# Two halves of the columns, two blocks of rows apart, in the second product of an MLP

## The chip, the cores and the metric

The kernel runs on one core of a Trainium2 chip. The metric is the time of one execution in device microseconds: 2081.96 us is the median of three runs (2080.67 to 2084.63).

## The reference, cut to what matters

The program is one encoder layer with 512 tokens and 2048 features, in float32: neighbourhood attention, and then an MLP, each behind an RMS norm and added to its input. The change touches the last line of the MLP only.

```python
def sq_relu_mlp(h, w1, w2):        # h: 512 x 2048, w1: 2048 x 8192, w2: 8192 x 2048
    a = jax.nn.relu(h @ w1)
    return (a * a) @ w2

x = x + sq_relu_mlp(rms_norm(x, norm_mlp[layer]), mlp_w1[layer], mlp_w2[layer])
```

## The kernel before, in words

Both products of the MLP are done in *units*, objects of class `Pair`. A unit makes 512 tokens x 1024 columns (two tiles of 512 columns) from four *blocks* of 512 rows of the weight. Each block is a 2 x 2 multiplication of quarters that is done with seven products instead of eight (the Strassen-Winograd scheme); the seven are numbered 1, 5, 6, 4 (first stage) and 2, 3, 7 (second stage). `Pair.chunks` gives the order: first stage of all blocks, then second stage of all blocks, 28 steps for four blocks. Each step takes one weight quarter of 128 x 1024 values and one *left side*, a combination of quarters of the left matrix. Both are kept as two float32r parts, a high one and the rest (h and l), and a step is 12 matmuls of 128 x 512: four places times hh, hl and lh (L248).

What a step needs of the other engines:

- The weight quarter (512 KB) is loaded by SP six steps ahead (`load_raw`, L193) into one of ten buffers. VectorE adds an earlier quarter for products 5, 6, 4 and 7 (L217). ScalarE makes the high part (L233) and VectorE the rest (L235), started three steps ahead.
- Products are summed in PSUM. When the last block of a product is done, `evict` takes its two banks to SBUF and adds the parts together (L265 to L274, L670, L672).

There are eight units h0 to h7 for the first product, and then eight for the second: y0_0, y0_1, y1_0, y1_1, y2_0, y2_1, y3_0, y3_1. The first number is one of four groups of four blocks (2048 rows of w2), the second is the half of the columns, called p. So both halves of the columns go through the same four blocks, one after the other.

The left sides of the second product are made from the hidden units' results. `take_hidden` scales and applies ReLU; eight *windows* of work follow in the next unit, one behind each second-stage step. A window transposes four squares on TensorE, ScalarE squares them, VectorE makes sums (L714 to L719), and POOL's queue writes them to DRAM (`z_t`, seven left sides of a block). `pass_on` brings them back: behind a step (m, b) of a unit, when the left side that this step used is not needed again, SP loads one left side (256 KB, L759, `zr`), and six sub-steps later (a step has four) ScalarE and VectorE split it (L554, L556). Before the change this is done in h7, y0_1, y1_1 and y2_1, for all 28 left sides of the next group; y0_0, y1_0, y2_0 and the units of group 3 make none. So 56 tiles of 128 x 512 hold left sides all the time, of 70 that the pool has.

A unit of the second product ends in eight quarters of 128 x 512. `take_out` lets POOL's queue add each of them into `y_sum` in DRAM with an accumulating DMA (L748). Only the last unit of either half loads `y_sum` (L732, called from the step with product 4 of the last block), adds it and writes the output.

The order of the work on each engine follows the program's order of issue: `later` and `start` put the side work of a step behind a number of sub-steps, and every engine and SP's queue work in order.

Of the kernel before, what the change touches and what calls it, by code (L numbers as in the profile page):

```python
# [17 lines left out]
P = 128  # L18
T = 512
D = 2048  # L20
# [5 lines left out]
NCH = HID // D  # L26
# [6 lines left out]
NB = KT // 4  # L33
# [8 lines left out]
STEP, WAIT, PAIR = 1, 5, 3  # L42


class Unit:
# [7 lines left out]
    def __init__(self, name, src, act, done, kind):  # L53
        self.name, self.src, self.act, self.done, self.kind = name, src, act, done, kind
        self.n = KT // 4 if kind == "narrow" else KT
        self.raw, self.parts, self.ps = {}, {}, None
        self.load, self.before, self.after, self.lag = None, None, None, 0


class Pair:  # L60
# [16 lines left out]
    QUARTER = {1: (0, 0), 5: (0, 1), 6: (1, 1), 4: (1, 0), 2: (1, 0), 3: (1, 1), 7: (0, 1)}  # L77
    CHAIN = {5: 1, 6: 5, 4: 6, 7: 3}

    def __init__(self, name, w, row, col, comb, take):  # L80
        self.name, self.w, self.row, self.col, self.comb, self.take = name, w, row, col, comb, take
        self.raw, self.parts, self.banks, self.after = {}, {}, {}, None
        self.t, self.u, self.p4, self.p5 = {}, {}, {}, {}

    def chunks(self):
        return [(self, (m, b)) for stage in (self.FIRST, self.SECOND) for b in range(NB) for m in stage]

    def quarter(self, m, b):
        r, c = self.QUARTER[m]
        r, c = self.row + (4 * b + 2 * r) * P, self.col + c * T  # L90
        return self.w[r // (2 * P), c // T]


# [1 line left out]
def natten_mlp_kernel(ctx, tc, x_t, gains, w_qk, w_v, bias, w_o, w1, w2, out_t):  # L95
    nc = tc.nc
# [8 lines left out]
    def wtile(name, dt=F32):  # L105
        return tiles.tile([P, T], dt, tag="w", name=name)

    def bank(name):
        return psum.tile([P, T], F32, tag="b", name=name)
# [11 lines left out]
    def pair(name):  # L121
        return wtile(f"{name}h", F32R), wtile(f"{name}l", F32R)
# [49 lines left out]
    def later(lag, fn):  # L172
        side.append((pos[0] + lag, fn))

    def start(steps):

        wait = next(steps, None)
        if wait is not None:
            later(wait, lambda: start(steps))

    def run_side(until):
        while True:
            due = sorted((s for s in side if s[0] <= until), key=lambda s: s[0])
            if not due:
                return
            for s in due:
                side.remove(s)
                s[1]()
# [48 lines left out]
    def multiply_pair(u, i):  # L237
        m, b = i
        x = u.BANK[m]
        if x not in u.banks:  # L240
            u.banks[x] = [bank(f"{x}_{u.name}_{j}") for j in range(2)]
        wh, wl = u.parts.pop(i)
        ah, al = u.comb[b][m]
        for k in range(2):
            for j in range(2):
                c = slice(k * HALF + j * P, k * HALF + (j + 1) * P)
                for n, (a, w) in enumerate(((ah, wh), (ah, wl), (al, wh))):
                    nc.tensor.matmul(out=u.banks[x][j], lhsT=a[:, c], rhs=w[:, k],  # L248
                                     start=(m in u.FIRST and b + k + n == 0), stop=(b == NB - 1 and k == 1 and n == 2),
                                     skip_group_check=True)  # L250
                pos[0] += 1
                if 2 * k + j < 3:
                    run_side(pos[0])
        if b == NB - 1:
            start(evict(u, m))
        if u.after is not None:
            u.after(m, b)
        run_side(pos[0])
# [148 lines left out]
    def v_done(g):  # L407
        def done(ps):
            vs[g] = [split(ps[j], f"v{g}_{j}", gain=r_mix[:, j:j + 1]) for j in range(QB)]
        return done  # L410

    class Head:
        def __init__(self, h):
            self.h = h
            self.p = {}
# [105 lines left out]
    for g in range(NG):  # L521
        u = Unit(f"v{g}", lambda i, g=g: w_v[i // 2, g], xa, v_done(g), "tokens")
# [24 lines left out]
    xc = [{} for _ in range(NB)]  # L547
    sq_a = wtile("sq_a")

    def parts_of(dst, m, src, name):  # L550

        h, l = pair(name)
        view = lambda z: z.rearrange("p (k n) -> p k n", k=2)
        nc.scalar.activation(view(h), src, AF.Copy)  # L554
        yield STEP
        nc.vector.tensor_tensor(out=view(l), in0=src, in1=view(h).bitcast(F32), op=ALU.subtract)  # L556
        dst[m] = (h, l)
        yield STEP
# [45 lines left out]
    def window():  # L604
        if windows:
            windows.pop(0)()
# [49 lines left out]
    for g in range(NG):  # L656
        u = Unit(f"o{g}", lambda i, g=g: w_o[i // 2, g], oa, o_done(g), "wide")
# [6 lines left out]
    FP = HID // (2 * T)  # L664

    z_t = [dram.tile([P, 7, 2, HALF], F32, name=f"z_{i}", tag=f"z_{i}") for i in range(2 * FP)]
# [8 lines left out]
    def take_hidden(p):  # L675
        zs = {}

        def take(c, half, src, add, minus=False):
            if add is None:
                t = wtile(f"z_{p}_{c}_{half}")  # L680
            else:
                t = join(src, add, minus)
                src = t
            nc.scalar.activation(t, src, AF.Relu, scale=r_a[:, c:c + 1])
            zs[c, half] = t
            if len(zs) == 8:
                for n in range(8):
                    windows.append(left_window(p, n // 4, n // 2 % 2, n % 2, zs))
        return take
# [35 lines left out]
    def take_out(p, last):  # L725
        ys = {}

        def prefetch():
            for c in range(QB):
                for half in range(2):  # L730
                    ys[c, half] = wtile(f"ys_{p}_{c}_{half}")
                    nc.sync.dma_start(out=ys[c, half], in_=y_sum[c, 2 * p + half])  # L732

        def take(c, half, src, add, minus=False):
            rows, cols = slice(c * P, (c + 1) * P), slice((2 * p + half) * T, (2 * p + half + 1) * T)
            if add is not None:
                if last:
                    nc.vector.tensor_tensor(out=add, in0=add, in1=ys[c, half], op=ALU.add)
                t = join(src, add, minus)
            elif last:  # L740
                t = join(src, ys[c, half], False)
            else:
                t = wtile(f"c_{p}_{c}_{half}")
                nc.scalar.activation(t, src, AF.Copy)
            if last:
                nc.sync.dma_start(out=out_t[rows, cols], in_=t)
            else:
                nc.gpsimd.dma_start(out=y_sum[c, 2 * p + half], in_=t, accum_op=ALU.add)  # L748
        return take, prefetch

    def pass_on(dst, block):


        order = (2, 4, 1, 5, 6, 3, 7)
        loaded = {}

        def load(m, b):
            t = loaded[m, b] = wtile(f"zr{m}_z{block}_{b}")
            nc.sync.dma_start(out=t.rearrange("p (k n) -> p k n", k=2), in_=z_t[4 * block + b][:, order.index(m)])  # L759

        def split_left(m, b):
            yield from parts_of(dst[b], m, loaded.pop((m, b)).rearrange("p (k n) -> p k n", k=2), f"a{m}_z{block}_{b}")

        def after(m, b):
            load(m, b)
            later(6 * STEP, lambda: start(split_left(m, b)))
        return after

    pairs, comb = [], xc
    for p in range(FP):  # L770
        u = Pair(f"h{p}", w1, 0, 2 * p * T, comb, take_hidden(p))
        pairs.append(u)
    zc = [[{} for _ in range(NB)] for _ in range(NCH)]
    for c in range(NCH):
        for p in range(2):
            take, prefetch = take_out(p, c == NCH - 1)
            u = Pair(f"y{c}_{p}", w2, c * D, 2 * p * T, zc[c], take)
            u.prefetch = prefetch if c == NCH - 1 else None
            pairs.append(u)
    for n, u in enumerate(pairs):  # L780
        hand = None
        if n >= FP - 1 and (n - FP + 1) % 2 == 0 and n < len(pairs) - 1:
            block = (n - FP + 1) // 2
            hand = pass_on(zc[block], block)

        def after(m, b, n=n, u=u, hand=hand):
            if m in u.SECOND:
                if n == 0 and m == 2 and b == 0:
                    start(norm_a())
                window()  # L790
            if m == 4 and b == NB - 1 and n >= FP and u.prefetch is not None:
                u.prefetch()
            if hand is not None:
                hand(m, b)
        u.after = after
        chunks += u.chunks()
# [54 lines left out]
```

## Time and profile before

| | before |
|---|---|
| median of three runs | 2081.96 us |
| profiled execution | 2081.29 us, span 2079.5 us, granted clock 0.995 |
| TensorE busy | 2044.1 us (98%) |
| TensorE's weight load busy | 1684.3 us (81%) |
| VectorE busy | 1546.5 us (74%) |
| ScalarE busy | 1045.5 us (50%) |
| POOL busy | 116.7 us (6%) |
| HBM | 348 MB read, 50 MB written, 192 GB/s |

The span is from the first to the last instruction. Weight loads overlap matmuls. The time of the engines beside TensorE counts only where TensorE waits for them.

### The profile page before, as it was taken

How to read it: one execution, taken by the hardware profiler on the slowest of the kernel's cores; microseconds unless marked ns; L12 is line 12 of the kernel's file. 1: busy time of each engine (PE TensorE's matmuls, PEld its weight loads, DVE VectorE, ACT ScalarE, POOL GpSimd, SP SyncE). 2: the span in 40 equal slices, each digit the busy share in tenths (PEclk: the TensorE clock that was granted, in tenths of full speed). 3: DMA queues.
4: the chain of work that ended last, by engine and by line, in shares of the span. 5: the costliest groups of instructions: out<-in, count | busy, mean ns of one | idle time of the engine just before them, and what ended most of it. 6: DMA issues, size and time to landing. Idle time of an engine off the chain costs nothing. (4 is left out here: it accounts for less than half of the span.)

```text
span 2079.5 us, 25226 instructions
## 1 busy us (share of the span) xinstructions
PE 2044.1 (98%) x9330; PEld 1684.3 (81%) x9330; DVE 1546.5 (74%) x1884; ACT 1045.5 (50%) x1412; POOL 116.7 (6%) x166
## 2 busy tenths in 40 slices
PE   9999999999999999999999999999989999999998
PEld 7888888888888888888888888887877877778787
DVE  6674674774774469778878878798879778779786
ACT  6663563653663445544545545565445445346333
POOL 0000000000000000010110110100201011010000
PEclk9999999999999999999999999999999999999999
DMA  7222222222233346565866757778689598688874
GB/s 289 101 92 83 100 92 92 96 90 96 99 101 127 112 137 211 193 217 199 274 202 226 269 180 255 270 255 304 226 295 286 187 272 279 204 261 278 256 243 147
DMA packets 127900, 400.15 MB, mean 192 GB/s; under 512 B 15008, under 2 KB 15008, under 8 KB 127776
## 3 DMA queue, kind: packets, MB, share of 16 engines
q1 hardware_dynamic: 110736, 352.37, 50.3%
q0 software_dynamic: 16896, 46.15, 7.8%
q8 instruction: 73, 1.20, 0.2%
q14 instruction: 51, 0.42, 0.1%
q10 hardware_dynamic: 144, 0.02, 0.0%
HBM read 348.14 MB, written 50.33 MB: 192 GB/s over the span
## 5 line engine op out<-in xcount | busy, mean ns | idle before, releaser
L233 ACT ACTIVATE wh_h<-w_h 128x1024 fp32r<-128x1024 f32 x224 | 237.6, 1060 | 275.0 <-PE y_h L248 83.7
L233 ACT ACTIVATE wh_y<-w_y 128x1024 fp32r<-128x1024 f32 x224 | 236.5, 1059 | 234.2 <-PE y_y L248 69.0
L235 DVE TENSOR_TENSOR wl_h<-w_h,wh_h 128x1024 fp32r<-128x1024 f32 x224 | 272.8, 1221 | 77.4 <-ACT wh_h L233 76.7
L235 DVE TENSOR_TENSOR wl_y<-w_y,wh_y 128x1024 fp32r<-128x1024 f32 x224 | 271.0, 1219 | 24.5 <-ACT wh_y L233 24.0
L217 DVE TENSOR_TENSOR w_y<-w_y,w_y 128x1024 f32<-128x1024 f32 x128 | 156.1, 1220 | 70.9 <-DMA w_y<-in_w 68.1
L217 DVE TENSOR_TENSOR w_h<-w_h,w_h 128x1024 f32<-128x1024 f32 x128 | 155.1, 1219 | 42.9 <-DMA w_h<-in_w 42.8
L235 DVE TENSOR_TENSOR wl_o<-w_o,wh_o 128x1024 fp32r<-128x1024 f32 x32 | 39.1, 1223 | 58.7 <-ACT wh_o L233 58.6
L233 ACT ACTIVATE wh_o<-w_o 128x1024 fp32r<-128x1024 f32 x32 | 33.9, 1059 | 80.0 <-PE mm_o L302 66.2
L233 ACT ACTIVATE wh_q<-w_q 128x1024 fp32r<-128x1024 f32 x32 | 34.0, 1062 | 77.8 <-PE mm_q L302 30.2
L235 DVE TENSOR_TENSOR wl_q<-w_q,wh_q 128x1024 fp32r<-128x1024 f32 x32 | 39.2, 1225 | 43.6 <-ACT wh_q L233 42.3
L235 DVE TENSOR_TENSOR wl_k<-w_k,wh_k 128x1024 fp32r<-128x1024 f32 x32 | 39.1, 1222 | 37.9 <-ACT wh_k L233 37.9
L233 ACT ACTIVATE wh_k<-w_k 128x1024 fp32r<-128x1024 f32 x32 | 34.0, 1062 | 50.8 <-PE mm_q L302 31.1
L233 ACT ACTIVATE wh_v<-w_v 128x1024 fp32r<-128x1024 f32 x31 | 32.8, 1058 | 47.4 <-PE mm_v L302 23.4
L235 DVE TENSOR_TENSOR wl_v<-w_v,wh_v 128x1024 fp32r<-128x1024 f32 x31 | 37.9, 1223 | 23.0 <-ACT wh_v L233 22.6
L600 POOL DMA_DIRECT2D y<-x1t_0s x4 | 2.3, 583 | 770.1 <-ACT x1t_0s L599 770.1
L711 POOL DMA_DIRECT2D z<-zt x32 | 17.7, 553 | 453.0 <-ACT zt L706 452.9
L554 ACT ACTIVATE a_z_0h<-zr_z 128x512 fp32r<-128x512 f32 x28 | 17.6, 627 | 50.4 <-DMA zr_z<-z 48.5
L509 ACT ACTIVATE t<-t,st 128x256 f32<-128x256 f32 x64 | 32.0, 501 | 10.6 <-DVE st L505 10.6
L706 ACT ACTIVATE zt<-zt 128x512 f32<-128x512 f32 x64 | 37.1, 580 | 0.0
L248 PE MATMUL y_y<-wl_y,a_z_1h 128*128 128x512 f32 x64 | 26.6, 416 | 8.4 <-DVE wl_y L235 8.4
L248 PE MATMUL z_y<-wl_y,a_z_0h 128*128 128x512 f32 x64 | 26.7, 418 | 6.8 <-DVE wl_y L235 6.8
L554 ACT ACTIVATE a_z_3h<-zr_z 128x512 fp32r<-128x512 f32 x28 | 17.5, 626 | 29.6 <-DMA zr_z<-z 29.6
(1435 smaller groups left out, 6304.2 us busy)
## 6 DMA issues: line engine op xcount, KB each, us to landing
w_h<-in_w SPq DMA_DIRECT2D x224, 512.0 KB, 4.3
w_y<-in_w SPq DMA_DIRECT2D x224, 512.0 KB, 4.6
zr_z<-z SPq DMA_DIRECT2D x112, 256.0 KB, 5.3
w_q<-in_w_qk SPq DMA_DIRECT2D x32, 512.0 KB, 3.5
w_k<-in_w_qk SPq DMA_DIRECT2D x32, 512.0 KB, 3.5
w_o<-in_w_o SPq DMA_DIRECT2D x32, 512.0 KB, 3.5
w_v<-in_w_v SPq DMA_DIRECT2D x31, 512.0 KB, 3.5
z<-zt POOLq DMA_DIRECT2D x32, 256.0 KB, 3.9
```

Source lines behind the costliest of these rows:

```text
L217: nc.vector.tensor_tensor(out=s, in0=s, in1=u.raw[u.CHAIN[m], b], op=ALU.add)
L233: kept(nc.scalar.activation(h, s, AF.Copy))
L235: kept(nc.vector.tensor_tensor(out=l, in0=s, in1=h.bitcast(F32), op=ALU.subtract))
L248: nc.tensor.matmul(out=u.banks[x][j], lhsT=a[:, c], rhs=w[:, k], start=(m in u.FIRST and b + k + n == 0), stop=(b == NB - 1 and k == 1 and ...
L509: nc.scalar.activation(halves[i], halves[i], AF.Exp, bias=st[:, i:i + 1], accum_out=st[:, 2 + i:3 + i])
L554: nc.scalar.activation(view(h), src, AF.Copy)
L600: nc.gpsimd.dma_start(out=dst, in_=t)
L706: nc.scalar.activation(t[:, i], ps, AF.Square)
L711: nc.gpsimd.dma_start(out=dst[:, 2], in_=t[:, 0, :HALF])
```

## The change

`Pair` gets a range of blocks instead of a first row, so a unit may have any blocks. The second product has nine units y0 to y8. Even ones do p = 1, odd ones p = 0. y0 has blocks 0 and 1, y1 blocks 0 to 3, y2 blocks 2 to 5, y3 blocks 4 to 7, and so on to y7 with blocks 12 to 15 and y8 with 14 and 15. Each unit thus uses two blocks for the last time, and behind their steps the left sides of two new blocks are made. h7 makes those of blocks 0 to 3 as before, but the ones of blocks 2 and 3 come 48 sub-steps (12 steps) later. y1 to y6 make two blocks' each. y0 has six second-stage steps; behind the two with product 7 it runs a second window. The last unit of either half is y7 or y8.

```diff
-        return [(self, (m, b)) for stage in (self.FIRST, self.SECOND) for b in range(NB) for m in stage]
+        return [(self, (m, b)) for stage in (self.FIRST, self.SECOND) for b in self.blocks for m in stage]
...
-        if b == NB - 1:
+        if b == u.blocks[-1]:
             start(evict(u, m))
...
-    def pass_on(dst, block):
+    def pass_on(heirs):
...
         def load(m, b):
-            t = loaded[m, b] = wtile(f"zr{m}_z{block}_{b}")
-            nc.sync.dma_start(out=t.rearrange("p (k n) -> p k n", k=2), in_=z_t[4 * block + b][:, order.index(m)])
+            t = loaded[m, b] = wtile(f"zr{m}_z_{b}")
+            nc.sync.dma_start(out=t.rearrange("p (k n) -> p k n", k=2), in_=z_t[b][:, order.index(m)])
...
         def after(m, b):
-            load(m, b)
-            later(6 * STEP, lambda: start(split_left(m, b)))
+            if b in heirs:
+
+                wait = 48 * STEP if heirs[b] == b >= 2 else 0
+                later(wait, lambda: load(m, heirs[b]))
+                later(wait + 6 * STEP, lambda: start(split_left(m, heirs[b])))
         return after
...
+    pairs = [Pair(f"h{p}", w1, range(NB), 2 * p * T, xc, take_hidden(p)) for p in range(FP)]
+    zc = [{} for _ in range(NCH * NB)]
+    for n in range(2 * NCH + 1):
+        p, c = 1 - n % 2, 2 * n - 2
+        rows = range(max(c, 0), min(c + NB, NCH * NB))
+        take, prefetch = take_out(p, n >= 2 * NCH - 1)
+        u = Pair(f"y{n}", w2, rows, 2 * p * T, zc, take)
+        u.prefetch = prefetch if n >= 2 * NCH - 1 else None
         pairs.append(u)
-    zc = [[{} for _ in range(NB)] for _ in range(NCH)]
-    for c in range(NCH):
-        for p in range(2):
-            take, prefetch = take_out(p, c == NCH - 1)
-            u = Pair(f"y{c}_{p}", w2, c * D, 2 * p * T, zc[c], take)
-            u.prefetch = prefetch if c == NCH - 1 else None
-            pairs.append(u)
     for n, u in enumerate(pairs):
-        hand = None
-        if n >= FP - 1 and (n - FP + 1) % 2 == 0 and n < len(pairs) - 1:
-            block = (n - FP + 1) // 2
-            hand = pass_on(zc[block], block)
+        c = 2 * (n - FP) - 2
+        if n == FP - 1:
+            hand = pass_on({b: b for b in u.blocks})
+        elif n > FP and c + NB < NCH * NB:
+            hand = pass_on({c: c + NB, c + 1: c + NB + 1})
+        else:
+            hand = None
 
         def after(m, b, n=n, u=u, hand=hand):
             if m in u.SECOND:
                 if n == 0 and m == 2 and b == 0:
                     start(norm_a())
                 window()
+                if n == FP and m == 7:
+                    window()
```

## Rows read from the trace of the kernel before

**Rows 1.** The page, busy time of TensorE, share of the span, instructions.

```profile
PE 2044.1 (98%) x9330; PEld 1684.3 (81%) x9330; DVE 1546.5 (74%) x1884; ACT 1045.5 (50%) x1412; POOL 116.7 (6%) x166
```

**Rows 2.** Timeline of TensorE: first matmuls of h6, h7, y0_0 to y3_1; the last.

```profile
1258.54 0.39 PE L248 MATMUL x_h<-wh_h,a_x0h 128*128 128x512 f32 x1
...
1338.59 0.39 PE L248 MATMUL x_h<-wh_h,a_x0h 128*128 128x512 f32 x1
...
1419.65 0.39 PE L248 MATMUL x_y<-wh_y,a_z_0h 128*128 128x512 f32 x1
...
1502.18 0.39 PE L248 MATMUL x_y<-wh_y,a_z_0h 128*128 128x512 f32 x1
...
1587.89 0.39 PE L248 MATMUL x_y<-wh_y,a_z_0h 128*128 128x512 f32 x1
...
1667.71 0.39 PE L248 MATMUL x_y<-wh_y,a_z_0h 128*128 128x512 f32 x1
...
1753.54 0.39 PE L248 MATMUL x_y<-wh_y,a_z_0h 128*128 128x512 f32 x1
...
1834.07 0.39 PE L248 MATMUL x_y<-wh_y,a_z_0h 128*128 128x512 f32 x1
...
1918.59 0.39 PE L248 MATMUL x_y<-wh_y,a_z_0h 128*128 128x512 f32 x1
...
1997.16 0.39 PE L248 MATMUL x_y<-wh_y,a_z_0h 128*128 128x512 f32 x1
...
2073.29 0.39 PE L248 MATMUL y_y<-wh_y,a_z_3l 128*128 128x512 f32 x1
```

**Rows 3.** Windows: y0_1's first 43.5 us, its rest, and y1_0's first 43.5 us.

```profile
core 0: us, PE busy (x) PEld busy (x) DVE busy (x) ACT busy (x) POOL busy (x), PEclk, DMA share, GB/s
1502.20:1545.70 43.50, 36.67 (x151) 29.51 (x150) 34.09 (x38) 19.65 (x24) 3.90 (x5) 0.92 0.97 308
1545.70:1587.90 42.20, 42.20 (x188) 34.92 (x187) 40.44 (x47) 26.21 (x34) 1.72 (x2) 1.00 0.86 281
1587.90:1631.40 43.50, 41.35 (x181) 33.48 (x180) 32.54 (x33) 18.29 (x19) 5.27 (x6) 1.00 0.79 241
```

**Rows 4.** Waits (us in total, times, longest) from 1667.7 to 1711, start of y1_1.

```profile
ACT a_z_0h L554 <- DMA zr_z<-z: 12.2, 3, 7.7
DVE w_y L217 <- DMA w_y<-in_w: 5.4, 1, 5.4
...
PE z_y L248 <- DVE wl_y L235: 4.2, 1, 4.2
...
DVE a_z_0l L556 <- ACT a_z_0h L554: 3.6, 1, 3.6
```

**Rows 5.** Waits from 1587.9 to 1631, start of y1_0.

```profile
DVE w_y L217 <- DMA w_y<-in_w: 9.0, 3, 4.0
```

**Rows 6.** Transfers by queue from 1583 to 1606: packets, MB, share of 16 engines.

```profile
q1 hardware_dynamic: 1515, 4.71, 54.6%
q0 software_dynamic: 1152, 2.10, 52.1%
```

**Rows 7.** Transfers by queue from 1463 to 1502, windows' writes in y0_0.

```profile
q0 software_dynamic: 1066, 3.62, 25.0%
```

**Rows 8.** One instruction, min/median/max ns (first three); group of lines, busy us, mean ns.

```profile
L235 DVE TENSOR_TENSOR wl_y<-w_y,wh_y x224: 1210/1218/1228, 1418.6 to 2066.6; 128x1024 fp32r<-128x1024 f32 x112
L217 DVE TENSOR_TENSOR w_y<-w_y,w_y x128: 1212/1219/1227, 1410.7 to 2052.2; 128x1024 f32<-128x1024 f32 x128
...
L556 DVE TENSOR_TENSOR a_z_0l<-zr_z,a_z_0h x28: 677/684/693, 1346.5 to 1901.6; 128x512 fp32r<-128x512 f32 x28
...
L714 DVE TENSOR_TENSOR zt_0s<-zt 128x256 f32<-128x256 f32 x2 | 0.8, 419 | 0.0
```

**Rows 9.** Windows of 3 us in y0_1, columns as in rows 3.

```profile
1527.00:1530.00 3.00, 3.00 (x9) 2.33 (x8) 3.00 (x4) 1.49 (x2) 0.00 (x0) 0.50 0.88 326
```

More of the change, by code (lines that the diff above doesn't have):

```diff
@@ L78, with __init__ @@
     CHAIN = {5: 1, 6: 5, 4: 6, 7: 3}
-    def __init__(self, name, w, row, col, comb, take):
-        self.name, self.w, self.row, self.col, self.comb, self.take = name, w, row, col, comb, take
+    def __init__(self, name, w, blocks, col, comb, take):
+        self.name, self.w, self.blocks, self.col, self.comb, self.take = name, w, blocks, col, comb, take
         self.raw, self.parts, self.banks, self.after = {}, {}, {}, None
@@ L85, in chunks @@
     def chunks(self):
-        return [(self, (m, b)) for stage in (self.FIRST, self.SECOND) for b in range(NB) for m in stage]
+        return [(self, (m, b)) for stage in (self.FIRST, self.SECOND) for b in self.blocks for m in stage]
     def quarter(self, m, b):
         r, c = self.QUARTER[m]
-        r, c = self.row + (4 * b + 2 * r) * P, self.col + c * T
+        r, c = (4 * b + 2 * r) * P, self.col + c * T
         return self.w[r // (2 * P), c // T]
@@ L248, in multiply_pair @@
                     nc.tensor.matmul(out=u.banks[x][j], lhsT=a[:, c], rhs=w[:, k],
-                                     start=(m in u.FIRST and b + k + n == 0), stop=(b == NB - 1 and k == 1 and n == 2),
+                                     start=(m in u.FIRST and b == u.blocks[0] and k + n == 0),
+                                     stop=(b == u.blocks[-1] and k == 1 and n == 2),
                                      skip_group_check=True)
@@ L757, in load @@
         def load(m, b):
-            t = loaded[m, b] = wtile(f"zr{m}_z{block}_{b}")
-            nc.sync.dma_start(out=t.rearrange("p (k n) -> p k n", k=2), in_=z_t[4 * block + b][:, order.index(m)])
+            t = loaded[m, b] = wtile(f"zr{m}_z_{b}")
+            nc.sync.dma_start(out=t.rearrange("p (k n) -> p k n", k=2), in_=z_t[b][:, order.index(m)])
         def split_left(m, b):
-            yield from parts_of(dst[b], m, loaded.pop((m, b)).rearrange("p (k n) -> p k n", k=2), f"a{m}_z{block}_{b}")
+            yield from parts_of(zc[b], m, loaded.pop((m, b)).rearrange("p (k n) -> p k n", k=2), f"a{m}_z_{b}")
@@ L764, in after @@
         def after(m, b):
-            load(m, b)
-            later(6 * STEP, lambda: start(split_left(m, b)))
-        return after
-    pairs, comb = [], xc
-    for p in range(FP):
-        u = Pair(f"h{p}", w1, 0, 2 * p * T, comb, take_hidden(p))
-        pairs.append(u)
-    zc = [[{} for _ in range(NB)] for _ in range(NCH)]
-    for c in range(NCH):
-        for p in range(2):
-            take, prefetch = take_out(p, c == NCH - 1)
-            u = Pair(f"y{c}_{p}", w2, c * D, 2 * p * T, zc[c], take)
-            u.prefetch = prefetch if c == NCH - 1 else None
-            pairs.append(u)
@@ L790, in after @@
                 window()
-            if m == 4 and b == NB - 1 and n >= FP and u.prefetch is not None:
+                if n == FP and m == 7:
+                    window()
+            if m == 4 and b == u.blocks[-1] and n >= FP and u.prefetch is not None:
                 u.prefetch()
```

## The prediction

> **What bounds the kernel now.** I read the page's busy shares first, then TensorE's timeline at the start of each unit, then the windows inside the units, and last the waits and transfers at the places where time is lost. TensorE is busy for 98% of the span [rows 1], so only what TensorE loses can come back, and whatever makes it lose more is paid in full.
>
> The unit starts say where it loses [rows 2]. The last unit, y3_1, runs its 336 matmuls in 76.13 us from first to last start, 0.227 us each: 76.36 us is an undisturbed unit without transposes and 2.73 us one of its 28 steps (12 matmuls). The hidden unit h6, with 32 transposes among its matmuls, takes 80.05 us; that is the measure for h7 and y0_0, which have as many. Against these, the losses are: h7 1.0, y0_0 2.5, y0_1 9.35, y1_0 3.45, y1_1 9.45, y2_0 4.15, y2_1 8.15, y3_0 2.2, y3_1 0: together 40.3 us. That is all the change can win.
>
> The three units that make left sides behind an accumulating unit (y0_1, y1_1, y2_1) lose 9.0 us in the mean; the three that only follow an accumulating unit (y1_0, y2_0, y3_0) lose 3.3. The windows say when in the unit it happens [rows 3]: in the first 43.5 us of y0_1, TensorE starts 151 matmuls where 192 fit (43.5 / 0.227), and in the next 42.2 us 188, all that fit. Yet the left sides go on through both halves. So VectorE and the transfers keep up with 28 left sides in a unit; what fails is the first part of it. The DMA share there is 0.97, against 0.79 at the start of y1_0 [rows 3].
>
> There two things meet. The unit before leaves eight quarters of y, each added into DRAM by an accumulating DMA, and the first left sides are fetched. In y1_1 the waits are on transfers: ScalarE on `zr_z`, VectorE's join on a raw weight, and TensorE then on VectorE's split [rows 4]. In y1_0, without left sides to make, VectorE waits for weights too, 9.0 us in three waits [rows 5], and TensorE loses less.
>
> The transfers can be added up. In the 23 us around the start of y1_0 the accumulating queue moves exactly one unit's eight quarters, 2.10 MB, for 52.1% of the 16 engines' time, and SP's queue 4.71 MB for 54.6% [rows 6]. That is 5.7 us per MB and 2.67 us per MB. So one unit's accumulation costs 12.0 us of all 16 engines, one weight quarter (0.524 MB) 1.4 us, one left side (0.262 MB) 0.7 us. In the first eight steps (21.8 us) weights take 11.2 us and accumulation 12.0: 23.2, over by 1.4. With eight left sides, 5.6 more, it is 28.8, over by 7.0. The extra 5.6 us is what the two kinds of start differ by (9.0 - 3.3 = 5.7). When TensorE has stood still for long in such a start its clock falls to half, and the restart pays for that too: 9 matmuls in 3 us where 13 fit, at 0.50 of the clock [rows 9]; this is inside the 9.0.
>
> **The change, part by part.**
> *Units.* The p = 1 columns are cut into 2, 4, 4, 4 and 2 blocks, the p = 0 columns into four times 4, so nine units y0 to y8 replace eight. Matmuls, weights and left sides stay the same in number. One more unit is evicted and accumulated: 12 VectorE and 4 ScalarE instructions and 8 accumulating DMAs. They run beside TensorE, and what they cost is the one more unit start behind an accumulation, counted below. Without TensorE's cover the VectorE part would be 12 x 0.68 = 8 us.
>
> *Left sides.* What matters is where they stand. Every step of a block in `heirs` fetches one, and the heirs are the unit's first two blocks. In each of y1 to y6 the left sides are therefore made in steps 1 to 8 and 17 to 22. Steps 9 to 16 and 23 to 28 are freed, but these lose nothing now. In steps 1 to 8 stand just as many fetches as in the heavy units of before, eight, beside the same accumulation. The heavy start of y0_1, y1_1, y2_1 occurs six times (y1 to y6) instead of three. The light start occurs once (y7) instead of three times.
>
> I price a heavy start at 9.0 us, the mean of three rows. From below it is bounded by the light start, 3.3 (the left sides hidden), from above by 9.45 for y2 to y6. y1 may be worse, see the next paragraph. Six heavy starts are 54.0, y7 is 3.3, y8 follows a unit that writes straight to the output, as y3_1 does, and loses 0.
>
> *h7 and y0.* h7 now makes 22 left sides, because those of blocks 2 and 3 come 12 steps later. The other six fall on y0's steps 7 to 12. All 8 transposing windows of h7's result, one behind each of y0_0's first eight second-stage steps before, now stand in y0's six second-stage steps, two of them on the last. VectorE has there 8 splits and joins (9.8 us), 4 left sides (2.7), 16 window steps (6.7) and the first stage's 6 evictions (4.1), 23.3 us [rows 8], where TensorE needs 6 x 2.73 + 3.9 = 20.3. It falls 3 us behind. Three steps of prepared weights cover some of it; I take 2 us, between 0 and 6. The left-side and weight fetches stand on the same SP queue, so a fetch that waits for a free tile holds the weights behind it; that is the upper end. The 3.62 MB that the windows write cost a quarter of 39 us [rows 7], 9.8 us of the engines, and now end right at y1's start; y0_1 had some calm steps between. I leave y1 at 9.0 and keep +5 for the range. The losses of h7 (1.0) and y0's start (2.5) stay.
>
> *Waits and ends.* The change adds no wait to an instruction. A fetch still stands on SP behind the same step and the split on ScalarE six sub-steps later; behind that split on ScalarE are the weights' splits, for which VectorE and then TensorE wait, as in rows 4. At the end y8 has 14 steps. Its eight loads of y come six steps before the end instead of twelve, some 11 us before the first is used. I count 0, with 3 us as the other end if they arrive late.
>
> **The sum.** Losses after: 1.0 + 4.5 + 54.0 + 3.3 + 0 = 62.8 us, against 40.3: 22.5 us more. The profiled execution took 2081.3 us (span 2079.5), 0.7 us below the median of the runs, so the change should take 2103.8, about 2104 us.
>
> A rule speaks against this sum. The Trainium skill (DMA: Bandwidth & Descriptors, "Anatomy of one DMA") prices the moving part of a transfer as its bytes over 436 GB/s, whatever the kind. By that the first eight steps would carry 8.39 MB in an estimated 19.2 us, under 21.8, and a heavy start would lose nothing to transfers. The rows of this trace disagree for accumulating transfers (5.7 us per MB is 175 GB/s [rows 6]); the second rival has the time that would follow if the transfers were not the limit.
>
> **The rivals.**
> *The left sides' cost is kept, not doubled.* If each left side carries its own delay wherever it stands, 84 of them cost 3 x 5.7 = 17.1 us before and after. Then the light start is paid by seven units, 7 x 3.3 = 23.1, and with h7 and y0 at 3.5 the losses are 43.7: 3.4 us more, 2084.7. For it: the sum of fetched bytes is unchanged. Against it: the second half of y0_1 has 12 left sides and loses nothing [rows 3].
>
> *VectorE is the limit, and the change takes it off.* In a heavy first stage four steps cost 7 x 1.22 + 4 x 0.68 = 11.3 us on VectorE against 10.9 on TensorE [rows 8]; with half the left sides it is 9.9. If this, and not the transfers, makes the 9.0, all six middle units lose only what a light one does: 1.0 + 2.5 + 7 x 3.3 = 26.6, so 13.7 us less, 2067.6: faster. It decides if the first eight steps of y2 to y6 lose under about 5 us each (40.3 = 4.5 + 3.3 + 3.5 + 29, over six units). For it: TensorE's direct waits are on VectorE. Against it: in y1_1's start VectorE sits idle for a weight and for ScalarE [rows 4], and it keeps up in the second half of y0_1 [rows 3].
>
> *y0 and y1 pile up.* If VectorE's 3 us, tile waits and the late writes add up, y0 and y1 lose 6 and 14 instead of 4.5 and 9: 2110.
>
> **How the numbers follow.** Chances: the forecast 0.62, the pile-up on top of it 0.06, kept cost 0.13, VectorE 0.19. The forecast's own range is 2092 to 2113. To leave out no more than 2 in 10, I reach from 2072, which takes in the kept cost and half-way to VectorE's case, to 2116. What a measurement can tell from no change is 0.2%, about 4 us. The kept cost falls inside that for the most part; so faster 0.19, same 0.12, slower 0.69.
>
> **What would show it.** In the changed kernel's trace, TensorE's starts of y1 to y6 should be 84 to 87 us apart, each with its loss in the first eight or nine steps, a DMA share near 1 and a dip of the granted clock there. Steps 9 to 16 should be clean, and y7 near 79.6. ScalarE's waits on `zr_z` should about double. I am wrong if the middle units are 80 us long, if the losses move to other steps, or if y0 is far over 45 us.

## The result, and the profile after

The changed kernel takes 2107.8 us (median of four runs, 2105.8 to 2108.9), the kernel before 2083.15 us beside it: ratio 1.0118, 95% interval 1.0101 to 1.0136. It is slower by 1.2%. The forecast was 2104.0, between 2072 and 2116.

The profiled execution took 2108.9 us (span 2107.1), 27.6 us more than before's 2081.3. Here is TensorE's timeline with the first matmul of h7, y0 to y8, and the last matmul, as in [rows 2].

```profile
1341.19 0.39 PE L248 MATMUL x_h<-wh_h,a_x0h 128*128 128x512 f32 x1
1422.69 0.39 PE L248 MATMUL x_y<-wh_y,a_z_0h 128*128 128x512 f32 x1
1466.15 0.48 PE L248 MATMUL x_y<-wh_y,a_z_0h 128*128 128x512 f32 x1
1554.41 0.39 PE L248 MATMUL x_y<-wh_y,a_z_2h 128*128 128x512 f32 x1
1638.77 0.39 PE L248 MATMUL x_y<-wh_y,a_z_4h 128*128 128x512 f32 x1
1723.25 0.39 PE L248 MATMUL x_y<-wh_y,a_z_6h 128*128 128x512 f32 x1
1809.20 0.39 PE L248 MATMUL x_y<-wh_y,a_z_8h 128*128 128x512 f32 x1
1891.22 0.39 PE L248 MATMUL x_y<-wh_y,a_z_10h 128*128 128x512 f32 x1
1977.08 0.39 PE L248 MATMUL x_y<-wh_y,a_z_12h 128*128 128x512 f32 x1
2062.94 0.39 PE L248 MATMUL x_y<-wh_y,a_z_14h 128*128 128x512 f32 x1
2100.79 0.39 PE L248 MATMUL y_y<-wh_y,a_z_15l 128*128 128x512 f32 x1
```

Taking off 76.36 us for 28 steps, 38.18 for 14 and 3.7 for a unit's 32 transposes, as in the prediction, the losses are those in the second line of the table below. They add up to 65.2 us, against 40.3 before: 24.9 us more. The other 2.6 us stand ahead of h7 (it starts at 1341.19 instead of 1338.59), in code that is the same. Run e4, whose code up to there is that of before, starts h7 at 1341.19 too, so this is a difference between executions. Step by step, 56.0 of the 63.8 us that y0 to y8 lose fall in the first eight steps of a unit (before: 35.3 of 39.3).

Losses of TensorE in us, unit by unit, worked out for each run from the unit starts in its trace. The runs e1 to e10 are told below. The heads name the changed kernel's units; in brackets are those of the kernel before, for before, e4 and e8.

| kernel | h7 | y0 (y0_0) | y1 (y0_1) | y2 (y1_0) | y3 (y1_1) | y4 (y2_0) | y5 (y2_1) | y6 (y3_0) | y7 (y3_1) | y8 | sum |
|---|---|---|---|---|---|---|---|---|---|---|---|
| before | 1.0 | 2.5 | 9.35 | 3.5 | 9.5 | 4.2 | 8.2 | 2.2 | 0 | | 40.3 |
| after | 1.45 | 1.6 | 11.9 | 8.0 | 8.1 | 9.6 | 5.7 | 9.5 | 9.5 | 0 | 65.2 |
| e1 fetches later | 1.2 | 1.3 | 12.3 | 7.7 | 6.0 | 7.3 | 5.6 | 7.1 | 3.5 | 0 | 51.8 |
| e2 no left sides | 0.4 | 1.6 | 10.2 | 8.05 | 11.05 | 9.4 | 10.0 | 11.0 | 6.2 | 0 | 67.9 |
| e3 adds kept | 0.6 | 1.9 | 9.8 | 1.05 | 1.4 | 1.6 | 1.1 | 2.15 | 0 | 0 | 19.3 |
| e4 before, adds kept | 0.7 | 2.2 | 7.95 | 0.4 | 1.65 | 2.5 | 3.0 | 4.4 | 0 | | 22.5 |
| e5 adds kept, fetches later | 0.2 | 2.0 | 6.65 | 1.2 | 1.0 | 1.3 | 1.3 | 1.4 | 0 | 0 | 14.7 |
| e6 adds kept, split later | 0 | 0.7 | 7.6 | 0 | 0 | 0 | 0 | 0 | 0 | 0 | 7.1 |
| e7 plain writes | 1.2 | 1.05 | 7.4 | 3.1 | 3.6 | 3.2 | 4.0 | 3.6 | 3.1 | 0 | 30.2 |
| e8 before, both mends | 0 | 0.8 | 2.0 | 0.6 | 0 | 0.6 | 0 | 0.6 | 0 | | 4.0 |
| e9 split later alone | 0 | 0 | 5.2 | 7.7 | 6.5 | 9.2 | 6.2 | 9.2 | 4.6 | 0 | 48.2 |
| e10 all three | 0 | 0.65 | 1.0 | 0 | 0 | 0 | 0 | 0 | 0 | 0 | 0.3 |

(Values between -0.2 and 0.05 are written as 0; the sums are of the unrounded ones.)

One unit does not fit the prediction at all: y7. It makes no left sides, should have been a light start with 3.3 us, and lost 9.5. The waits of its first 43.5 us:

```profile
ACT wh_y L233 <- PE z_y L248: 14.4, 3, 7.0
DVE w_y L217 <- DMA w_y<-in_w: 10.9, 4, 5.9
...
PE z_y L248 <- DVE wl_y L235: 5.9, 2, 3.6
```

No left side is among them. VectorE stands 10.9 us for raw weights in the add of two quarters (L217). Its own timeline (start, length, what, idle before it and releaser) shows what this wait does:

```profile
1987.01 1.21 DVE L217 TENSOR_TENSOR w_y<-w_y,w_y 128x1024 f32<-128x1024 f32 x1
1988.14 1.22 DVE L235 TENSOR_TENSOR wl_y<-w_y,wh_y 128x1024 fp32r<-128x1024 f32 x1
1989.28 1.22 DVE L217 TENSOR_TENSOR w_y<-w_y,w_y 128x1024 f32<-128x1024 f32 x1
1996.43 1.22 DVE L217 TENSOR_TENSOR w_y<-w_y,w_y 128x1024 f32<-128x1024 f32 x1 [5.93 <-DMA w_y<-in_w]
1997.57 1.22 DVE L235 TENSOR_TENSOR wl_y<-w_y,wh_y 128x1024 fp32r<-128x1024 f32 x1
```

And SP's issue of the weight for which it waits, with the microseconds from that issue to its landing:

```profile
1987.11 0.33 SPq L193 DMA_DIRECT2D w_y<-in_w  x1
```

```profile
w_y<-in_w SPq DMA_DIRECT2D x1, 512.0 KB, 9.2
```

1987.11 + 9.2 = 1996.3: the add waits for a load that was issued 3.4 us before VectorE came to it (1996.43 - 5.93 = 1990.50). Yet SP has weights issued ten buffers ahead: at 1992 us, 27 loads and 37 splits (L235) are still to come. So the add is not for the weight that TensorE needs next, it is for one some eight steps later, and the split that TensorE needs stands behind it (1997.57). In VectorE's queue, counted in the order of the trace, the number of splits between an add and the split of the same weight, for the 16 adds of a unit in order, is:

```
before  y0_1   3 3 3 4 2 2 3 3 3 3 3 3 5 7 8 6
before  y1_0   7 7 7 7 7 7 4 4 5 6 6 6 8 8 8 8
before  y1_1   8 8 7 8 8 8 8 6 6 7 7 7 7 7 8 6
after   y1     4 4 3 1 1 1 1 1 1 1 1 2 4 6 8 7
after   y3     8 7 7 8 8 8 8 6 6 7 7 7 7 8 8 7
after   y7     8 7 7 8 8 8 8 6 6 8 8 7 8 8 8 6
e1      y3     7 7 7 7 7 8 6 6 6 7 7 7 8 8 8 6
e2      y3     8 8 7 8 8 8 8 6 6 8 8 7 8 8 8 8
e3      y3     1 1 1 1 1 1 1 1 1 1 1 1 1 1 3 4
e9      y3     7 7 7 8 8 8 5 5 5 6 6 6 8 8 8 7
```

The kernel's text issues an add three steps ahead; the scheduler that orders each engine's instructions had moved it up. I had read before's order of work from the text; what is said of it ahead of the prediction holds for the text alone. The waits of rows 4 and 5 on raw weights are waits of the same adds (L217). The light starts of before differ in this order too. VectorE at the start of y1_0:

```profile
1586.60 0.68 DVE L556 TENSOR_TENSOR a_z_2l<-zr_z,a_z_2h 128x512 fp32r<-128x512 f32 x1
1587.20 1.28 DVE L672 TENSOR_TENSOR u_y<-z_y,u_y 128x512 f32<-128x512 f32 x2
1588.40 1.21 DVE L235 TENSOR_TENSOR wl_y<-w_y,wh_y 128x1024 fp32r<-128x1024 f32 x1
...
1592.53 1.22 DVE L235 TENSOR_TENSOR wl_y<-w_y,wh_y 128x1024 fp32r<-128x1024 f32 x1
...
1594.26 1.22 DVE L235 TENSOR_TENSOR wl_y<-w_y,wh_y 128x1024 fp32r<-128x1024 f32 x1
...
1596.00 1.21 DVE L235 TENSOR_TENSOR wl_y<-w_y,wh_y 128x1024 fp32r<-128x1024 f32 x1
1597.14 1.21 DVE L217 TENSOR_TENSOR w_y<-w_y,w_y 128x1024 f32<-128x1024 f32 x1
```

From 1586.6 to 1597.1, while the accumulation starts, four splits go by without an add between them. In y1_0 and y1_1 alike, the first six adds are done before the unit starts. The seventh stands four splits ahead of its own in y1_0 and comes 9.3 us into the unit; in y1_1 it stands eight ahead and comes after 4.9 us, in y2_1 after 3.3, and in y2 to y7 of the changed kernel after 2.7 to 4.6. Why the scheduler orders one unit this way and another that way is not shown.

Two units are of another kind: y0_1 before and y1 after, whose first adds stand only one to four ahead (table). Lines from the waits of their first 43.5 us, y0_1 first:

```profile
ACT a_z_0h L554 <- DMA zr_z<-z: 14.6, 3, 11.0
...
PE y_y L248 <- ACT wh_y L233: 5.6, 1, 5.6
```

```profile
ACT a_z_4h L555 <- DMA zr_z<-z: 15.3, 3, 7.6
...
PE w_y L248 <- ACT wh_y L233: 4.5, 2, 3.3
```

Here TensorE waits for ScalarE's high part of a weight (`wh_y`), and ScalarE stands at the split of a left side (L554, in the changed kernel L555) that has not landed, up to 11.0 us at one. The windows of rows 3 and 9, from which the prediction reasoned, show y0_1.

### The profile page after: what moved, and what is told of

It reads as the page before. It is cut to its first block, busy times and chain, and to the rows that moved or that the text cites. A ratio compares the mean times of both kernels' runs of the same rounds, so it can differ in the third digit from the quotient of the medians.

```text
span 2107.1 us, 25249 instructions
## 1 busy us (share of the span) xinstructions
PE 2056.1 (98%) x9330; PEld 1690.4 (80%) x9330; DVE 1553.6 (74%) x1896; ACT 1046.7 (50%) x1416; POOL 123.9 (6%) x174
## 4 chain that ended last, share of the span: by engine, by line
PE 44%; issue 32%; DMA 12%; DVE 8%; POOL 3%; ACT 1%; SPq 0%; DVEq 0%; POOLq 0%; ACTq 0%
PE mm_v L303 8%; PE mm_q L303 8%; PE mm_k L303 8%; DMA w_y<-in_w 8%; PE mm_o L303 5%; DMA zr_z<-z 4%; DVE wl_y L235 4%; PE z_y L248 3%; PE y_y L248 3%; PE x_y L248 2%; DVE w_y L217 2%; PE w_y L248 2%; PE o L470 1%; POOL z L722 1%; POOL z L711 1%
## 5 line engine op out<-in xcount | busy, mean ns | idle before, releaser
L235 DVE TENSOR_TENSOR wl_h<-w_h,wh_h 128x1024 fp32r<-128x1024 f32 x224 | 272.9, 1221 | 80.8 <-ACT wh_h L233 79.9
L235 DVE TENSOR_TENSOR wl_y<-w_y,wh_y 128x1024 fp32r<-128x1024 f32 x224 | 271.0, 1219 | 22.5 <-ACT wh_y L233 22.4
L217 DVE TENSOR_TENSOR w_y<-w_y,w_y 128x1024 f32<-128x1024 f32 x128 | 156.2, 1221 | 82.9 <-DMA w_y<-in_w 82.3
L217 DVE TENSOR_TENSOR w_h<-w_h,w_h 128x1024 f32<-128x1024 f32 x128 | 155.1, 1219 | 43.5 <-DMA w_h<-in_w 43.4
L235 DVE TENSOR_TENSOR wl_o<-w_o,wh_o 128x1024 fp32r<-128x1024 f32 x32 | 39.1, 1223 | 58.4 <-ACT wh_o L233 58.3
L233 ACT ACTIVATE wh_q<-w_q 128x1024 fp32r<-128x1024 f32 x32 | 34.0, 1062 | 77.8 <-PE mm_q L303 30.2
L235 DVE TENSOR_TENSOR wl_q<-w_q,wh_q 128x1024 fp32r<-128x1024 f32 x32 | 39.2, 1225 | 43.7 <-ACT wh_q L233 42.4
L235 DVE TENSOR_TENSOR wl_k<-w_k,wh_k 128x1024 fp32r<-128x1024 f32 x32 | 39.1, 1222 | 37.9 <-ACT wh_k L233 37.9
L235 DVE TENSOR_TENSOR wl_v<-w_v,wh_v 128x1024 fp32r<-128x1024 f32 x31 | 37.9, 1224 | 24.3 <-ACT wh_v L233 24.0
L712 POOL DMA_DIRECT2D z<-zt x32 | 17.8, 556 | 439.4 <-ACT zt L707 439.1
L749 POOL DMA_DIRECT2D y<-c x14 | 12.2, 894 | 417.1 <-ACT c L745 416.2
L711 POOL DMA_DIRECT2D z<-zt x32 | 23.4, 730 | 71.5 <-ACT zt L707 70.3
L248 PE MATMUL z_h<-wh_h,a_x0h 128*128 128x512 f32 x64 | 25.7, 402 | 0.0
L248 PE MATMUL z_h<-wh_h,a_x1h 128*128 128x512 f32 x64 | 25.7, 402 | 0.0
```

What stands on the lines that cost most here:

```text
L217: nc.vector.tensor_tensor(out=s, in0=s, in1=u.raw[u.CHAIN[m], b], op=ALU.add)
L233: kept(nc.scalar.activation(h, s, AF.Copy))
L235: kept(nc.vector.tensor_tensor(out=l, in0=s, in1=h.bitcast(F32), op=ALU.subtract))
L711: nc.gpsimd.dma_start(out=dst[:, 0:2], in_=t[:, 1].rearrange("p (m n) -> p m n", m=2))
L712: nc.gpsimd.dma_start(out=dst[:, 2], in_=t[:, 0, :HALF])
```

## The experiments

The theory of the prediction (*transfers*) was that eight left-side fetches beside an accumulation make a heavy start. The rival formed from y7 (*order*): late landings cost only what stands behind the waiting instruction in an engine's queue, and VectorE's adds stand so far ahead that they wait for loads just issued.

**e1, fetches later.**

```diff
-                wait = 48 * STEP if heirs[b] == b >= 2 else 0
+                wait = 48 * STEP if heirs[b] == b >= 2 else 32 * STEP if heirs[b] != b and m in Pair.FIRST else 0
```

> The changed kernel, with the first-stage left sides of y1 to y6 fetched and split eight steps later (steps 9 to 16 instead of 1 to 8), so that no left side meets the accumulation at the start of a unit. The transfer theory (fetches and accumulation together ask for more than the 16 engines have): the starts of y1 to y6 lose about 3.3 us each instead of 5.7 to 11.9, some 2077 us. The order theory (VectorE's adds of weight quarters stand up to 8 splits ahead of the splits that TensorE waits for, so VectorE waits for weights that were issued just before, whatever the left sides do): y2 to y6 still lose 7 to 9.5 us each, 2098 to 2108 us.

Measured: 2096.0 us, ratio to before 1.0054 (1.0034 to 1.0075). y1 to y6 still lose 5.6 to 12.3, y7 3.5; the time is a little below what the order theory said and far above the transfer theory's. It is a weaker test than it was meant to be. In the trace, SP issues eight first-stage fetches for y3: in the changed kernel two of them in the last step of y2 and six in y3's first eight steps, here still two and two. By step, y1 to y6 lose 3.3 to 5.7 us in their first eight steps, instead of 5.0 to 10.5, and the rest later. The edit also moved the adds (the seventh of a unit stands six ahead instead of eight). So the starts get lighter, and e1 cannot say by which of the two.

**e2, no left sides.**

```diff
-        elif n > FP and c + NB < NCH * NB:
-            hand = pass_on({c: c + NB, c + 1: c + NB + 1})
...
-        ah, al = u.comb[b][m]
+        ah, al = u.comb[b % NB][m]
```

> The changed kernel with no left sides made in y1 to y6: the sixteen blocks use the left sides of blocks 0 to 3 again (the rest of the second product's left sides is left out). Transfer theory: y1 to y7 are light starts, 3.3 us each, about 2070 us. Order theory: the adds still stand 8 ahead, and y2 to y7 lose 7 to 9.5 us each although no left side is fetched, 2093 to 2105 us.

Measured: 2109.9 us, 1.0126 (1.0108 to 1.0144). Taking away 84 fetches and 84 splits gained nothing, and the time is even above the order theory's. y2 to y6 lose 8 to 11 us and y7 6.2 with only weights and the accumulation on the engines, so a heavy start needs no fetch. The adds of a unit stand as far ahead as in y7 of the changed kernel or a little further (table). VectorE's adds (count, busy, mean ns, idle before them and releaser) wait twice as long as in before, 138.6 us against 68.1:

```profile
L217 DVE TENSOR_TENSOR w_y<-w_y,w_y 128x1024 f32<-128x1024 f32 x128 | 156.4, 1223 | 141.5 <-DMA w_y<-in_w 138.6 <-DVE p_y L269 1.1 <-issue 1.1
```

**e3 and e4, adds kept in order**, in the changed kernel and in the one before:

```diff
-                nc.vector.tensor_tensor(out=s, in0=s, in1=u.raw[u.CHAIN[m], b], op=ALU.add)
+                add = nc.vector.tensor_tensor(out=s, in0=s, in1=u.raw[u.CHAIN[m], b], op=ALU.add)
+                if u.name[0] == "y":
+                    tc.keep_in_program_order(add)
```

> The changed kernel with each add of weight quarters in the second product kept in the order of issue on VectorE, so it stands one split ahead of its own split and not up to 8; transfers, splits and left sides are the same. Transfer theory: y1 to y6 lose what they lose now, y7 goes to 3.3 us, about 2101 us. Order theory: the starts of y2 to y7 lose 1 to 4 us each instead of 5.7 to 9.6, 2070 to 2082 us.

> The kernel before with each add of weight quarters in the second product kept in the order of issue on VectorE. Transfer theory: no change beyond 3 us, 2080 to 2086 us. Order theory: y1_1 and y2_1 lose 1 to 4 us instead of 8.2 and 9.5, y1_0, y2_0 and y3_0 under 2.5, about 2068 us.

Measured: e3 2061.8 us, 0.9896 (0.9877 to 0.9914), 46 us less than the changed kernel; e4 2062.7 us, 0.9896 (0.9875 to 0.9917). Both fell further than expected. y2 to y6 of e3 lose 1.1 to 2.2 and y7 nothing. What stays is y1 with 9.8, and in e4 y0_1 with 7.95 and y3_0 with 4.4 (under 2.5 was expected): the adds do not explain these. The adds' waits for weights in e3:

```profile
L217 DVE TENSOR_TENSOR w_y<-w_y,w_y 128x1024 f32<-128x1024 f32 x128 | 155.9, 1218 | 0.0
```

The transfers are the same in number and stand at nearly the same steps (five fetches in y3's first eight steps, against six). y2 of e3, window of its first 43.5 us (columns as in rows 3), loses 1 us with a DMA share of 0.90 and the granted clock at full speed.

```profile
1551.30:1594.80 43.50, 43.14 (x188) 34.70 (x187) 39.38 (x42) 22.36 (x26) 4.04 (x5) 1.00 0.90 279
```

**e5, adds kept and fetches later** (the edits of e3 and e1).

> The changed kernel with the adds kept in order (2061.8 us, y1 loses 9.8 us, y2 to y6 1.1 to 2.2 each), and the first-stage left sides of y1 to y6 eight steps later. If what is left in y1 is ScalarE standing at the split of a left side that has not landed while the engines are full, y1 falls to about 3 us and the time to 2052 to 2056. If y1's loss is transfers of weights alone, it stays near 9 and the time within 3 us of 2062.

Measured: 2058.4 us, 0.9874 (0.9848 to 0.99). y1 falls from 9.8 to 6.65, between the two expectations, and the time too; not decided by it.

**e6, adds kept and split later.**

```diff
-                later(wait + 6 * STEP, lambda: start(split_left(m, heirs[b])))
+                later(wait + 12 * STEP, lambda: start(split_left(m, heirs[b])))
```

> The changed kernel with the adds kept in order, and every left side's split twelve sub-steps behind its fetch instead of six (fetches unmoved). If ScalarE's wait at a left side that has not landed makes what is left, its waits on zr_z go from some 60 us to under 15, y1 loses about 4 us instead of 9.8, 2053 to 2057 us. If the engines' load alone makes it, no change: 2060 to 2064 us.

Measured: 2049.7 us, 0.9831 (0.9809 to 0.9853), 12 us below e3. The gain is there, but not where I put it: ScalarE's waits on left sides only go from 74 to 49 us, y1 only to 7.6; y2 to y6, which lost 7.3 us together in e3, lose nothing at all. The fetches moved a little with the splits (four in y3's first eight steps). In y3 (window of its first 43.5 us, then the transfers of its first 21.8 us: packets, MB, share; us to landing) the transfer engines are as full as in e3:

```profile
1624.20:1667.70 43.50, 43.50 (x194) 36.02 (x193) 40.78 (x44) 21.84 (x25) 4.09 (x5) 1.00 0.91 290
```

```profile
q1 hardware_dynamic: 1595, 4.77, 58.2%
q0 software_dynamic: 1089, 1.97, 49.2%
...
w_y<-in_w SPq DMA_DIRECT2D x8, 512.0 KB, 9.6
zr_z<-z SPq DMA_DIRECT2D x4, 256.0 KB, 9.6
...
y<-p_y POOLq DMA_DIRECT2D x2, 256.0 KB, 15.7
```

The queues ask for 58.2 + 49.2 = 107% of the engines (e3, the same stretch of y3: 56.7 + 50.9), a weight takes 9.6 us to land, and TensorE starts 194 matmuls where 192 fit by my pitch. With weights issued ten buffers ahead none of it reaches TensorE there; no run has fewer buffers.

**e7, plain writes** in the changed kernel, adds not kept:

```diff
-                nc.gpsimd.dma_start(out=y_sum[c, 2 * p + half], in_=t, accum_op=ALU.add)
+                nc.gpsimd.dma_start(out=y_sum[c, 2 * p + half], in_=t)
```

> The changed kernel (adds not kept) with the accumulating DMAs of y0 to y6 turned into plain writes of the same bytes from the same queue, so the parts of y are not summed. If the accumulation is what makes the weights land late at the starts, the weights land in about 3.5 to 5 us there, VectorE's waits for weights fall from 82 us to under 50, and y2 to y7 lose under 4 us each: 2065 to 2080 us. If the order of the adds alone costs it, whatever the transfers do, the time stays over 2098 us.

Measured: 2071.75 us, 0.9936 (0.9915 to 0.9957). y2 to y7 lose 3.1 to 4.0 each. Each engine's queue and SP's have the same order as in the changed kernel, so only the kind of transfer differs. In y3's first 21.8 us a weight lands in 5.3 us instead of 8.6. The adds still wait 70 us for weights, more than expected, in shorter pieces (3.4 us at most, 5.9 in the changed kernel). So most of the late landing comes from the accumulation; the order turns it into lost time.

**e8, before with both mends** (adds kept, split twelve sub-steps behind the fetch).

> The kernel before with both mends: adds kept in the order of issue and each left side's split twelve sub-steps behind its fetch. It tells what the change is worth once neither VectorE nor ScalarE waits for transfers. If the halved left sides bring nothing then (VectorE keeps up with 28 in a unit), it is within 4 us of the changed kernel with both mends (2049.7): 2046 to 2054 us. If VectorE is short in units with 28 left sides, those lose some 4 us each more: 2058 to 2066 us.

Measured: 2046.0 us, 0.9827 (0.9814 to 0.9841). The changed kernel with the same mends (e6) has 0.9831 (0.9809 to 0.9853). This is what was expected if the halved left sides bring nothing, and the two cannot be told apart: with both mends, the change is worth nothing that these runs can tell. Of what e4 left, y0_1 goes from 7.95 to 2.0 and y3_0 from 4.4 to 0.6.

**e9, split later alone**, adds not kept, in the changed kernel:

> The changed kernel with the splits of the left sides twelve sub-steps behind their fetch, the adds not kept. If the adds alone make the loss, no change: 2103 to 2110 us. If ScalarE's wait at the left sides were the larger part, 2075 to 2085 us.

Measured: 2091.9 us, 1.0047 (1.0033 to 1.006). A miss for both: 16 us less than the changed kernel, of which 6.7 in y1. ScalarE's waits on left sides go from 133 to 95 us. In y1 the adds stood close already, so there the gain is ScalarE's. In y2 to y7 the edit also moved the adds (the seventh five ahead instead of eight, table), and the rest cannot be put down to ScalarE alone.

**e10, all three** (adds kept, split later, fetches later).

> The changed kernel with the adds kept, the splits twelve sub-steps behind, and the first-stage fetches of y1 to y6 eight steps later. y2 to y8 have nothing left to lose (0 each with the first two mends); if the eight fetches at y1's start are what overfills the engines there, y1 falls from 7.1 us to under 4 and the time to 2046 to 2048 us; if the windows' writes and the accumulation do it without them, it stays at 2049 to 2052.

Measured: 2044.4 us, 0.9821 (0.9807 to 0.9834), losses of 0.3 us from h7 to the end. y1 falls from 7.6 to 1.0, as expected if its fetches count, and the time lies below the range. In the trace, seven fetches stand in y1's steps 3 to 9 in e6 and four in its steps 7 to 10 here, with the windows' writes and the accumulation still beside them. It is the fastest kernel of the study, 63 us below the changed one by the medians; its interval overlaps that of e8, though.

## Why the prediction was right or wrong

- *Where the time is lost.* Right: TensorE's stalls at the starts of units behind an accumulation decide. From h7 on TensorE loses 24.9 us more than before, 20.7 of them in the first eight steps of the units. Steps 9 to 16 are clean (0.6 us at most), and the DMA share (0.84 to 1.02 in the first 43.5 us of y1 to y6) and the granted clock there (0.92 to 0.96) are as said. Other signs failed: the starts of y1 to y6 are 82.0 to 88.3 us apart instead of 84 to 87, ScalarE's waits on `zr_z` went from 108 to 133 us instead of doubling, and y7 is 85.9 us long instead of 79.6.
- *y1 to y6, six heavy starts of 9.0.* The sum is right, 52.8 us against 54.0, for a reason that is not. I named the eight fetches (5.6 us of the engines) as what makes a start heavy. e2 has none of them and loses 8 to 11 us at y2 to y6; e3 has nearly all of them, asks for as much of the engines and loses 1.1 to 2.2. Shown instead, by e3 and e4 for y2 to y6: VectorE's adds, placed six to eight splits ahead of their own, standing still for weights that the accumulation delays (e7).
- *y1.* It is not of that kind: e3 leaves it 9.8 of its 11.9 us. There ScalarE stands at the split of a left side six sub-steps behind its fetch. Splitting later takes 6.7 us off by itself (e9), and with adds and splits mended, later fetches take off 6.6 more (e6, e10). So in this one unit it does cost that the fetches come beside the other transfers, by way of ScalarE's wait.
- *y7, a light start of 3.3.* Wrong: 9.5. This is where the failed step shows. It took the difference of 5.7 us between two groups of three units for the cost of what one of them did, while the groups also differed in the order of VectorE's queue, and y0_1 lost by ScalarE. With the adds kept (e3), y7 loses nothing.
- *The total.* That 2104.0 came within 3.8 us of 2107.8 is luck: y7 lost 6.2 us more than I counted and y1 2.9 more, y2 to y6 4.1 less and y0 2.9 less.
- *28.8 us of transfers in 21.8.* The engines are asked for more than they have, but for 107% (e6), not 28.8 / 21.8 = 132%. The conclusion does not hold: in e6 y2 to y7 hide it, with weights issued ten buffers ahead and adds and splits standing later in their queues.
- *The rule on bytes over 436 GB/s* (the Trainium skill, DMA: Bandwidth & Descriptors, "Anatomy of one DMA"). The Trainium skill gives it there for a DMA of the gpsimd path; I had used it for both queues. The trace of e6 disagrees as rows 6 did: 6.74 MB in 21.8 us are 309 GB/s with more than the engines' whole share asked for. That these starts lose nothing, as the rule would have it, has another reason.
- *y0.* 1.6 us instead of 4.5: the transposing windows and VectorE's 23.3 us in six steps cost nothing by themselves. (Its 20.3 us for TensorE count 3.9 for the transposes; h6 gives 3.7.) That the windows' late writes make y1 worse is not shown: e10 has them too and loses 1.0 in y1. The +5 kept for y1 was in place.
- *VectorE as the limit.* That rival asked the right question of the wrong quantity. VectorE's amount of work is no limit (e6 and e8 are equal), its order is.
- *Waits and ends.* y8 lost nothing and the end was hidden, as counted. "Adds no wait to an instruction" was true of the text, not of the queues: the adds' waits for weights went from 68 to 82 us.

## What to carry to other kernels

When engines work in order, read for each wait not only what it waits for but what stands behind it, and take the order from the queues as built, not from the text. A load that is waited for a few microseconds after its issue, while many buffers are ahead, is a sign that the instruction stands too early in its queue. Read from the trace whether an experiment moved only what it was meant to move: e1, e6 and e9 moved other things with it. And two groups of units that differ in one thing may differ in another, here in the order of a queue: look for a unit that has the one without the other before putting a price on it.

## What the runs showed of the hardware

An accumulating DMA of 256 KB lands in 9.9 us (median of the last quarters of a unit, changed kernel), the plain write of the same bytes in 5.5 (e7), with the same issues from the same queue. The transfers of POOL's queue in the first 21.8 us of y3 (packets, MB, share of 16 engines), first accumulating, then plain:

```profile
q0 software_dynamic: 897, 1.63, 46.3%
```

```profile
q0 software_dynamic: 480, 1.57, 21.0%
```

That is 6.2 us of the 16 engines per MB against 2.9, and nearly twice the packets for about the same bytes. Beside accumulation, a weight of 512 KB takes 7 to 10 us to land; the attention's weights of the same size, loaded before any accumulation, land in 3.5 (median, changed kernel).
